# Rounded weight and remainder interleaved element by element in SBUF

## The chip, the core and the metric

The kernel runs on one core of a Trainium2 chip. The metric is device time in microseconds of one execution; lower is better. A core has five engines with queues of their own: TensorE (PE) multiplies matrices, and loads its weights by separate instructions, which the profile lists as PEld; VectorE (DVE), ScalarE (ACT) and GpSimd (POOL) work element by element on 128 partitions; SyncE (SP) here only issues DMA transfers. SBUF is the on-chip memory that all of them read, PSUM takes the results of TensorE.

## What is computed

One layer of a decoder for 256 prompt tokens and 8 single decode tokens, together 264 columns, with a model width of 2048 and a feed-forward width of 5632. Everything is fp32.

```python
x = x + concat(RGLRU_group(xn), mLSTM_group(xn)) @ w_out      # xn = rmsnorm(x); inputs from xn @ w_in
xq = rmsnorm(x, g_xa) @ w_xa_q                                # cross attention, 4 heads, 256 memory tokens
s  = einsum('blhd,bmhd->bhlm', xq, mk) * 512 ** -0.5          # prompt: mk = mn @ w_k, mv = mn @ w_v
x  = x + (softmax(s) @ mv) @ w_xa_o                           # decode: mk, mv from caches
xf = rmsnorm(x, g_ffn)
x  = x + (silu(xf @ w_ffn_gate) * (xf @ w_ffn_up)) @ w_ffn_down
y  = rmsnorm(x, g_final)
```

The states of the two groups and the memory's keys and values are outputs too. Most of the arithmetic is in the projections, the products with w_in, w_out, w_xa_q, w_k, w_v, w_xa_o, gate, up and down.

## The kernel before

Activations lie with the features on the partitions: a chunk is 128 features by 264 tokens. The weight is the stationary operand of a projection, a block of 128 by 128 numbers, and the activations stream past it. TensorE multiplies fp32 in one pass only in a rounded format (fp32r), so each operand is split in two: a rounded part (h) and a remainder (l). `mm3` (line 179) then makes three matmuls for each chunk, weight h by activation h, weight h by activation l, weight l by activation h, and each of them loads its weights anew.

The program is a list `steps`. One step is usually one output block of 128 features: 2048 weights on each partition (16 blocks of 128), one DMA of 1 MB into `raw` (three buffers, issued by SP three steps ahead), a split, 48 matmuls into one PSUM bank. `split_half` (line 150) splits 1024 columns of the next step: ScalarE copies them to `wh`, which rounds, and VectorE subtracts `wh` from `raw` into `wl`. `wh` and `wl` are separate tiles with four buffers each, so the halves of two steps are in SBUF. `W` (line 169) hands `mm3` the 128 columns of a block from both tiles, contiguous in each. The very first step is split in parts of 256 and 512 columns. In the last part of the down projection a step has 1536 columns, and its second half 512.

Two kinds of step differ. `split_gates` and `pe_if` (lines 506 and 517) take only 64 columns of each block, put rounded part and remainder side by side in one block, and use each block for two matmuls. `pe_v` (line 1034) computes the memory's values with tokens on the partitions: there activations are the weights of the array and w_v, in pieces of 512 columns, is the moving operand; it has 16 steps.

Beside the projections runs side work, written as generators (`rg_gen`, `ml_gates`, `ml_heads`, `dec_k`, `dec_v`, `attend` and others), which `pump` advances between steps by estimated engine clocks. A scheduler then sets the order on PE, VectorE, ScalarE and POOL; the splits have high priority. SP's order is as written. POOL issues the DMAs of the caches (`kcT`, `vcT`, lines 966 and 970) and of outputs, and makes one subtraction (line 977) for each decode token and head.

The stages follow in this order: w_in (41 steps, gates among them), w_out (16), w_q (16), for each of four heads w_k (4) and w_v (4), w_o (16), gate and up (88), down (48, in three parts between them). Nearly all instructions are recorded under line 60, a helper's, so they are told apart by tiles: `mm<-B,wh` is a matmul with a rounded weight into a bank named mm. The small operations that the prediction uses are `evac_rgx` (line 407, eight numbers written with a step of four elements), `evac_q` (line 946, eight adjacent ones into `qsm`), and the two writers of `den` (lines 697 and 732, two adjacent numbers, and four with a step of three).

Of the kernel before, what the change touches and what calls it, by code (L numbers as in the profile page):

```python
# [10 lines left out]
F32 = mybir.dt.float32  # L11
F32R = mybir.dt.float32r
I32 = mybir.dt.int32
AF = mybir.ActivationFunctionType
# [3 lines left out]
P = 128  # L18
# [62 lines left out]
def layer_kernel(ctx: ExitStack, tc, xT, memT, vec, wrg, w_in, w_out, w_q, w_k, w_v, w_o,  # L81
# [3 lines left out]
    act, dve, pe = Engine(nc.scalar, price_act), Engine(nc.vector, price_dve), Engine(nc.tensor, price_pe)  # L85
# [3 lines left out]
    sb = ctx.enter_context(tc.tile_pool(name="sb", bufs=1))  # L89
# [6 lines left out]
    def nm(s):  # L96
        uid[0] += 1
        return f"{s}_{uid[0]}"

    def B(shape, dt=F32):  # L100
        return sb.tile(shape, dt, tag="B", bufs=NB, name=nm("B"))
# [35 lines left out]
    steps = []  # L137
    LD, LS = 3, 1

    raws, splits = {}, {}  # L140

    def load_piece(i):
        if i >= len(steps) or i in raws:
# [6 lines left out]
    def split_half(i, h, parts=1):  # L150
        if i >= len(steps):
            return
        if steps[i][2] is pe_if:
            if h == 0:
                split_gates(i)
            return
        cols = steps[i][1]
        lo, hi = h * 1024, min(cols, (h + 1) * 1024)
        wh = sb.tile([P, 1024], F32R, tag="wh", bufs=4, name=nm("wh"))
        wl = sb.tile([P, 1024], F32R, tag="wl", bufs=4, name=nm("wl"))  # L160
        r = raws[i]
        n = (hi - lo) // parts
        with tc.high_priority():
            for o in range(0, hi - lo, n):
                st["split"] = act.activation(wh[:, o: o + n], r[:, lo + o: lo + o + n], AF.Copy)
                dve.tensor_sub(wl[:, o: o + n], r[:, lo + o: lo + o + n], wh[:, o: o + n])
        splits[i, h] = (wh, wl)

    class W:
        def __init__(self, i):  # L170
# [15 lines left out]
    st = {}  # L186
# [48 lines left out]
    def bank(tag="mm"):  # L235
        return psm.tile([P, 512], F32, tag=tag, bufs=4, name=nm(tag))
# [269 lines left out]
    def split_gates(i):  # L506

        r = raws[i]
        for h in range(2):
            w = sb.tile([P, 8, P], F32R, tag="wh", bufs=4, name=nm("wh"))  # L510
            x = r[:, h * 1024: h * 1024 + 1024].rearrange("p (c m) -> p c m", m=P)
            with tc.high_priority():
                act.activation(w[:, :, 0:64], x[:, :, 0:64], AF.Copy)
                dve.tensor_sub(w[:, :, 64:128], x[:, :, 0:64], w[:, :, 0:64].bitcast(F32))
            splits[i, h] = w
# [303 lines left out]
    def proj(src, rhs, evac, cols=2048, n=N, need=()):  # L819

        def f(i):
            ps = bank()
            w = W(i)
            nch = cols // P
            for c in range(nch):
                mm3(ps[:, :n], w(c), rhs(c), c == 0, c == nch - 1)
            return ps
        steps.append((src, cols, f, evac, need))
# [191 lines left out]
    def evac_k(h, j):  # L1020
        def f(ps):
            if j == 0:
                kv["k", h] = HL(4, T)
            t = tmp(T)
            act.activation(t, ps[:, :T], AF.Copy)
            pool_e.dma_start(o_k[:, 4 * h + j, :], t)
            kh, kl = kv["k", h](j)
            act.activation(kh, ps[:, :T], AF.Copy)
            dve.tensor_sub(kl, ps[:, :T], kh.bitcast(F32))
            if j == 3:  # L1030
                st["att", h] = side(attend(h), 1)
        return f

    def pe_v(h, k4):
        def f(i):
            if k4 == 0:
                kv["vps"] = [bank(), bank()]
            w = W(i)
            for c in range(4):
                kc = k4 * 4 + c  # L1040
                mh, ml_ = rm(kc)
                wh, wl = w(c, 512)
                for tb in range(2):
                    ps = kv["vps"][tb]
                    s = slice(tb * P, tb * P + P)
                    pe.matmul(ps, mh[:, s], wh, start=(kc == 0), stop=False)
                    pe.matmul(ps, mh[:, s], wl, start=False, stop=False)
                    pe.matmul(ps, ml_[:, s], wh, start=False, stop=(kc == KC - 1))
            return kv["vps"]
        return f  # L1050

    def evac_vm(h):
        def f(vps):
            vv = B([P, 2, 512], F32R), B([P, 2, 512], F32R)
            kv["v", h] = vv
            vf = B([P, 2, 512])
            for tb in range(2):
                vh = vv[0][:, tb, :]
                act.activation(vh, vps[tb], AF.Copy)
                dve.tensor_sub(vv[1][:, tb, :], vps[tb], vh.bitcast(F32))  # L1060
                act.activation(vf[:, tb, :], vps[tb], AF.Copy)
                pool_e.dma_start(o_v[tb * P: tb * P + P, h * 512: h * 512 + 512], vf[:, tb, :])
            kv["vn"] = h + 1
        return f
# [57 lines left out]
    for h in range(H):  # L1122
        for j in range(4):
            proj(w_k[4 * h + j], rm, evac_k(h, j), n=T, need=("memg",))
        for k4 in range(4):
            steps.append((w_v[h, k4], 2048, pe_v(h, k4), evac_vm(h) if k4 == 3 else None, ()))

    def ro(c):
        return st["o"](c)
# [84 lines left out]
    r = sb.tile([P, 2048], F32, tag="raw", bufs=3, name=nm("raw"))  # L1214
# [10 lines left out]
    with tc.high_priority():  # L1225
        for c in range(KC):
            split(*xn(c), xres[:, c, :], V("g_mix", c))
            if c == 1:
                split_half(0, 0, 4)
            elif c == 3:  # L1230
                split_half(0, 1, 2)

    pend = []
    for i, (src, cols, pef, evf, need) in enumerate(steps):
# [12 lines left out]
        now = pe.clock  # L1247
        dve.clock, act.clock = max(dve.clock, now), max(act.clock, now)
        split_half(i + LS, 0)
        if i + LS < len(steps) and steps[i + LS][1] > 1024:  # L1250
            split_half(i + LS, 1)
# [17 lines left out]
    for lo, hi in ((0, 1), (1, 2), (2, 4), (4, 6), (6, 8), (8, 10), (10, 12), (12, 14), (14, 16)):  # L1269
        for c in range(lo, hi):  # L1270
            e, r = (pool_e, rstd) if c in POOLC else (dve, fin["ps"][:, :N])
# [108 lines left out]
```

## Time and profile before

| | |
|---|---|
| median of 2 runs | 1575.51 us (1574.54 and 1576.49) |
| the profiled execution's own time | 1576.51 us |
| its span, first to last instruction | 1574.8 us |
| mean granted TensorE clock | 0.991 |
| PE, PEld busy | 1556.5 us, 1532.6 us |
| VectorE, ScalarE busy | 1051.4 us, 789.7 us |
| rounding of weights on ScalarE, 1024 columns | 494 times, 1060 ns |
| remainder on VectorE, 1024 columns | 494 times, 1226 ns |

A group's row reads: line, engine, operation, output and inputs by name, shapes, count; then busy time in us and the mean of one in ns; then the engine's idle time before them and who ended it. Matmuls are pipelined: the record of one is longer than the distance to the next, so the pace is read from counts in a stretch, and records are only compared with each other. A row of a stretch gives its length, then for PE, PEld, VectorE, ScalarE and POOL the busy time with the number of instructions, then the granted clock, the DMA engines' share, and GB/s.

### The profile page before, as it was taken

The page shows a single profiled execution, that of the slowest core. Times are in us where ns is not written, and L with a number is a line of the kernel's source. Part 1 is how long each engine was busy: PE and PEld are TensorE (multiplying, and loading weights), DVE is VectorE, ACT ScalarE, POOL GpSimd, SP SyncE. Part 2 cuts the span into 40 slices and gives each one's busy share as a digit, 9 for nine tenths or more (in the row PEclk, how much of TensorE's full clock was granted, in tenths as well). Part 3 has the DMA queues.
Part 4 walks back from the last instruction along what each step waited for, and adds up shares of the span by engine and source line. Part 5 has one row for each costly group of instructions (what it writes and reads, how often), then busy time and mean ns, then how long its engine had stood idle before and what let it go on. Part 6 is the DMA issues. An engine that isn't in the chain of part 4 may idle for free.

```text
span 1574.8 us, 29829 instructions
## 1 busy us (share of the span) xinstructions
PE 1556.5 (99%) x12340; PEld 1532.6 (97%) x12340; DVE 1051.4 (67%) x2021; ACT 789.7 (50%) x1252; POOL 109.6 (7%) x174
## 2 busy tenths in 40 slices
PE   9999999999999999999999999999999999999997
PEld 8999999999999889999999999999999999999997
DVE  7876877787699899956655555455555554555554
ACT  7465675565455656645444444333444433344463
POOL 0001210000124333200000000000000000000000
PEclk9999999999999999999999999999999999999998
DMA  8455875546689788745545555555455554555452
GB/s 304 161 174 172 294 269 205 178 145 245 248 321 346 302 305 319 251 161 178 187 164 185 188 180 175 181 188 186 174 179 186 187 181 172 184 188 184 156 179 99
DMA packets 55303, 325.97 MB, mean 207 GB/s; under 512 B 6688, under 2 KB 7120, under 8 KB 24448
## 3 DMA queue, kind: packets, MB, share of 16 engines
q1 hardware_dynamic: 39744, 270.68, 48.4%
q0 software_dynamic: 15136, 53.16, 9.4%
q8 instruction: 96, 1.57, 0.4%
q14 instruction: 39, 0.32, 0.1%
q10 hardware_dynamic: 288, 0.23, 0.1%
HBM read 312.78 MB, written 11.28 MB: 206 GB/s over the span
## 4 chain that ended last, share of the span: by engine, by line
PE 94%; DMA 2%; DVE 2%; ACT 1%; issue 1%; DVEq 0%; POOL 0%; SPq 0%; ACTq 0%
PE mm L60 89%; PE ax L60 4%; DVE B L60 1%; DMA o_sc<-B 1%; ACT B L60 1%; DMA raw<-w_in 1%; ACT wh L60 0%; DMA B<-scr 0%; DVE wl L60 0%; ACT L60 0%; DMA vecs<-vec 0%; DMA scr<-lt 0%; DVE t L60 0%; DVE dw L60 0%; ACT t L60 0%
## 5 line engine op out<-in xcount | busy, mean ns | idle before, releaser
L60 PE MATMUL mm<-B,wh 128*128 128x264 f32 (+1 forms) x7520 | 1379.0, 285 | 4.8 <-DVE B L60 3.0
L60 PEld LDWEIGHTS mm<-B,wh 128*128 128x128 f32 x7520 | 1168.4, 189 | 6.4 <-ACT cso L60 3.1
L60 PE MATMUL mm<-B,wl 128*128 128x264 f32 (+1 forms) x3744 | 1062.8, 284 | 0.6 <-DVE wl L60 0.6
L60 ACT ACTIVATE wh<-raw 128x1024 fp32r<-128x1024 f32 (+2 forms) x518 | 536.9, 1038 | 692.0 <-PE mm L60 574.6
L60 DVE TENSOR_TENSOR wl<-raw,wh 128x1024 fp32r<-128x1024 f32 (+2 forms) x516 | 619.0, 1201 | 356.7 <-ACT wh L60 350.0
L60 PEld LDWEIGHTS mm<-B,wl 128*128 128x128 f32 x3744 | 706.7, 189 | 1.1 <-DVE wl L60 1.0
L60 DVE TENSOR_TENSOR t<-mm,rstd 128x264 f32<-128x264 f32 x104 | 44.9, 432 | 60.2 <-PE mm L60 60.2
L60 PE MATMUL mm<-wh,B 128*128 128x512 f32 x256 | 82.3, 395 | 0.0
L60 DVE TENSOR_TENSOR xres<-xres,mm 128x264 f32<-128x264 f32 x80 | 34.2, 428 | 47.1 <-PE mm L60 47.1
L1272 POOL TENSOR_TENSOR B<-B,rstd 128x264 f32<-128x264 f32 x4 | 2.8, 743 | 864.9 <-ACT rstd L60 864.9
L60 PEld LDWEIGHTS mm<-wh,B 128*128 128x128 f32 x256 | 47.8, 189 | 9.8
L60 DVE SCALAR_TENSOR_TENSOR B<-B,dw 128x256 f32<-128x256 f32 x128 | 52.6, 465 | 2.3 <-ACT dw L60 2.3
L60 PE MATMUL mm<-wl,B 128*128 128x512 f32 x128 | 50.6, 395 | 0.0
L60 DVE SCALAR_TENSOR_TENSOR dw<-B,qsm,dw 128x256 f32<-128x256 f32 x96 | 47.9, 500 | 1.4 <-ACT dw L60 0.7
L60 PE MATMUL ax<-B,B 128*128 128x256 f32 (+3 forms) x288 | 48.2, 308 | 0.3 <-DVE B L60 0.3
L60 PEld LDWEIGHTS ax<-B,B 128*128 128x128 f32 x288 | 40.8, 189 | 4.0 <-issue 1.2
L977 POOL TENSOR_TENSOR ds<-dw,ds 128x256 fp32r<-128x256 f32 x32 | 35.4, 1107 | 115.3 <-ACT ds L60 115.2
L60 ACT ACTIVATE B<-xres,vecs 128x264 fp32r<-128x264 f32 (+1 forms) x64 | 31.1, 503 | 2.5 <-DMA xres<-xT 1.4
L60 ACT ACTIVATE t<-xres 128x264 f32<-128x264 f32 x60 | 23.9, 413 | 15.4 <-DVE xres L60 15.4
L60 PEld LDWEIGHTS mm<-wl,B 128*128 128x128 f32 x128 | 24.1, 188 | 5.0
L966 POOL DMA_DIRECT2D B<-kcT x32 | 17.5, 546 | 147.4 <-DVE B L60 127.0
L60 DVE TENSOR_TENSOR acc_x<-acc_x,t 128x264 f32<-128x264 f32 x59 | 25.2, 428 | 0.9 <-ACT t L60 0.5
(157 smaller groups left out, 740.0 us busy)
## 6 DMA issues: line engine op xcount, KB each, us to landing
raw<-w_gu SPq DMA_DIRECT2D x88, 1024.0 KB, 4.8
raw<-w_in SPq DMA_DIRECT2D x40, 1024.0 KB, 4.9
raw<-w_d SPq DMA_DIRECT2D x32, 1024.0 KB, 4.8
raw<-w_out SPq DMA_DIRECT2D x16, 1024.0 KB, 4.8
B<-kcT POOLq DMA_DIRECT2D x32, 512.0 KB, 6.1
raw<-w_q SPq DMA_DIRECT2D x16, 1024.0 KB, 5.0
B<-vcT POOLq DMA_DIRECT2D x32, 512.0 KB, 7.2
raw<-w_k SPq DMA_DIRECT2D x16, 1024.0 KB, 6.4
```

Of the source, the lines that this page charges most:

```text
L60: return f(*a, **k)
L966: pool_e.dma_start(kc, kcT[h, b])
L977: pool_e.tensor_sub(ws[:, 1], acc, ws[:, 0].bitcast(F32))
L1272: e.tensor_mul(st["y"](c), st["y"](c), r)
```

## The change

`wh` and `wl` become one tile `w` of 2048 columns with four buffers, in which rounded part and remainder alternate: element 2k is the rounded part of weight k, element 2k + 1 its remainder. ScalarE writes every second element, VectorE reads the rounded part at a step of two elements and writes its result at a step of two, and each weight load for `mm3` takes 128 elements out of 256, a step of 8 bytes. The steps of w_v are marked `wide` and keep two contiguous parts in the tile. The gates keep their contiguous blocks, in the first half of a tile. The space is the same: four buffers of 8 KB a partition in place of four and four of 4 KB.

```diff
-    raws, splits = {}, {}
+    raws, splits, wide = {}, {}, set()
...
-        wh = sb.tile([P, 1024], F32R, tag="wh", bufs=4, name=nm("wh"))
-        wl = sb.tile([P, 1024], F32R, tag="wl", bufs=4, name=nm("wl"))
+        wt = wtile()
         r = raws[i]
+        if i in wide:
+            splits[i, h] = wt[:, 0:1024], wt[:, 1024:2048]
+            with tc.high_priority():
+                act.activation(wt[:, 0:1024], r[:, lo: hi], AF.Copy)
+                dve.tensor_sub(wt[:, 1024:2048], r[:, lo: hi], wt[:, 0:1024].bitcast(F32))
+            return
+
+        wt = wt.rearrange("p (k t) -> p k t", t=2)
+        wh, wl = wt[:, :, 0], wt[:, :, 1]
         n = (hi - lo) // parts
         with tc.high_priority():
             for o in range(0, hi - lo, n):
-                st["split"] = act.activation(wh[:, o: o + n], r[:, lo + o: lo + o + n], AF.Copy)
-                dve.tensor_sub(wl[:, o: o + n], r[:, lo + o: lo + o + n], wh[:, o: o + n])
+                xo = r[:, lo + o: lo + o + n]
+                st["split"] = act.activation(wh[:, o: o + n], xo, AF.Copy)
+                dve.tensor_sub(wl[:, o: o + n], xo, wh[:, o: o + n].bitcast(F32))
         splits[i, h] = (wh, wl)
+
+    def wtile():
+        return sb.tile([P, 2048], F32R, tag="w", bufs=4, name=nm("w"))
...
-            w = sb.tile([P, 8, P], F32R, tag="wh", bufs=4, name=nm("wh"))
+            w = wtile()[:, 0:1024].rearrange("p (c m) -> p c m", m=P)
...
         for k4 in range(4):
             steps.append((w_v[h, k4], 2048, pe_v(h, k4), evac_vm(h) if k4 == 3 else None, ()))
+            wide.add(len(steps) - 1)
```

The number of instructions on each engine stays the same, 12195 on PE among them, and SP's order too. The scheduler moves a few rows on the other engines. On PE, the first place is the transposes of the gates' columns (`ax<-ident`), which stand between the matmuls of two steps of w_in. Before:

```order
L60 MATMUL ax_1661<-B_884,ident 128x16 x3
L60 MATMUL ax_1661<-ident,B_966 128x4 x2
L60 MATMUL mm_1600<-B_126,wh_1520 128x264
L60 MATMUL mm_1600<-B_127,wh_1520 128x264
L60 MATMUL ax_1661<-ident,B_966 128x4 x3
L60 MATMUL ax_1749<-ident,B_1284 128x128 x4
L60 MATMUL mm_1528<-B_162,wl_1443 128x264
```

And now:

```order
L60 MATMUL ax_1623<-B_866,ident 128x16 x3
L60 MATMUL ax_1623<-ident,B_946 128x4 x3
L60 MATMUL mm_1562<-B_126,w_1486 128x264
L60 MATMUL mm_1562<-B_127,w_1486 128x264
L60 MATMUL ax_1623<-ident,B_946 128x4 x2
L60 MATMUL ax_1709<-ident,B_1256 128x128 x4
L60 MATMUL mm_1492<-B_160,w_1409 128x264 x2
```

One transpose of the five has moved ahead of the two matmuls of the next step.

On POOL, the place is the stage of w_k and w_v, where the caches of the decode tokens are loaded (`kcT`, `vcT`) and the decode queries' products are split (`ds`). Before:

```order
L966 DMA B_5847<-kcT 128x1024
L977 TENSOR_TENSOR ds_5601<-dw_5600,ds_5601 128x256
L970 DMA B_5851<-vcT 128x1024
L977 TENSOR_TENSOR ds_5684<-dw_5683,ds_5684 128x256
L966 DMA B_5936<-kcT 128x1024
L970 DMA B_5940<-vcT 128x1024
L966 DMA B_6019<-kcT 128x1024
L977 TENSOR_TENSOR ds_5767<-dw_5766,ds_5767 128x256
```

And now:

```order
L978 DMA B_5707<-kcT 128x1024
L989 TENSOR_TENSOR ds_5467<-dw_5466,ds_5467 128x256
L982 DMA B_5711<-vcT 128x1024
L989 TENSOR_TENSOR ds_5548<-dw_5547,ds_5548 128x256
L989 TENSOR_TENSOR ds_5629<-dw_5628,ds_5629 128x256
L978 DMA B_5794<-kcT 128x1024
L982 DMA B_5798<-vcT 128x1024
L978 DMA B_5875<-kcT 128x1024
```

One subtraction has moved ahead of the loads of the next pair. What follows from such pairs on VectorE stands up to two steps earlier or later from there on, and at the same step as before again towards the end of the stage.

## The prediction

> **What bounds the kernel now.** I read the page's engine table and its chain first, then the groups of instructions with their shapes kept apart, then a table by stretch of the span, and last the timeline of a microsecond where weight loads can be seen without long matmuls beside them. The page:
>
> ```profile
> span 1574.8 us, 29829 instructions
> PE 1556.5 (99%) x12340; PEld 1532.6 (97%) x12340; DVE 1051.4 (67%) x2021; ACT 789.7 (50%) x1252; POOL 109.6 (7%) x174
> PE 94%; DMA 2%; DVE 2%; ACT 1%; issue 1%; DVEq 0%; POOL 0%; SPq 0%; ACTq 0%
> ```
>
> TensorE is the bound: matmuls are under way in 99% of the span, and 94% of the chain that ended last lies on PE. But PEld, the weight loads, is at 97% too, so the page does not yet say whether a matmul's stream or the load in front of it sets the pace. The reader should see in the next rows what one of each takes.
>
> ```profile
> L60 PE MATMUL mm<-B,wh 128*128 128x264 f32 x7008 | 1286.0, 285 | 4.1 <-DVE B L60 3.0 <-ACT wh L60 1.1
> L60 PE MATMUL mm<-B,wh 128*128 128x256 f32 x512 | 93.1, 281 | 0.6 <-ACT B L60 0.5
> L60 PE MATMUL mm<-wh,B 128*128 128x512 f32 x256 | 82.3, 395 | 0.0
> ...
> L60 PEld LDWEIGHTS mm<-B,wh 128*128 128x128 f32 x7520 | 1168.4, 189 | 6.4 <-ACT cso L60 3.1 <-ACT wh L60 1.4 <-ACT B L60 1.1
> L60 PEld LDWEIGHTS mm<-B,wl 128*128 128x128 f32 x3744 | 706.7, 189 | 1.1 <-DVE wl L60 1.0
> ...
> L60 PEld LDWEIGHTS ax<-B,wh 128*128 128x128 f32 x64 | 10.8, 208 | 2.5 <-ACT wh L60 2.0 <-DVE B L60 0.2
> L60 PEld LDWEIGHTS ax<-B,wl 128*128 128x128 f32 x32 | 6.3, 203 | 0.0
> ```
>
> ```profile
> 760.00:1550.00 790.00, 790.00 (x6527) 790.00 (x6526) 435.43 (x543) 336.47 (x408) 0.00 (x0) 1.00 0.51 179
> ```
>
> That stretch (in order: us, PE, PEld, DVE, ACT and POOL busy, each with its instructions, clock, DMA share) holds W_o and the feed-forward part. 790 us over 6527 matmuls is one every 121.0 ns. From 256 to 512 columns a matmul grows from 281 to 395 ns, 0.445 ns a column; 264 columns stream for 117 ns. So the stream explains 117 of the 121 ns. What the load needs shows where the matmuls between loads are one column long:
>
> ```profile
> 37.55 0.76 PEld L60 LDWEIGHTS ax<-ones,acc_x 128*128 128x128 f32 x6
> 37.67 0.72 PE L60 MATMUL ax<-ones,acc_x 128*128 128x1 f32 x6
> ```
>
> Six loads run in 0.76 us, and one record is 0.19 us long, so they start (0.76 - 0.19) / 5 = 0.114 us apart with nothing to stream. A weight load of 128 contiguous fp32 columns therefore takes up to 114 ns, and it lies under a stream of 117 ns in a slot of 121. Both are nearly equal; the load has about 7 ns to spare. That is the point on which this change turns.
>
> **The change, part by part.** It adds and removes no instruction. It alters the address pattern of three kinds.
>
> First, the weight loads. Strided are all loads of projections: the four rows above give 7520 + 3744 + 64 + 32 = 11360, less 32 of the gates' step (16 chunks, two matmuls each), whose weights stay contiguous: 11328. The 384 matmuls that take W_v as the moving operand read contiguous halves as before. Each load now steps 2 elements, 8 bytes. No load in the trace has such a step, so I bound it. From below: nothing, for it is hidden unless it grows by over 7 ns, and a gain is limited to what the stream does not explain, 121 - 117 = 4 ns, 45 us over all loads. From above, the nearest rows are small VectorE operations that differ in the step of the result alone: the same product of PSUM and rstd, written to adjacent places (qsm), and to every fourth element (the history rows of line 407, "B").
>
> ```profile
> L60 DVE TENSOR_TENSOR qsm<-mm,rstd 128x8 f32<-128x8 f32 x16 | 2.5, 154 | 0.0
> L60 DVE TENSOR_TENSOR B<-mm,rstd 128x8 f32<-128x8 f32 x6 | 1.0, 160 | 0.0
> ```
>
> 6 ns over 8 elements is 0.75 ns an element with a step of 16 bytes. On 128 weights that is 96 ns, so the load would need 210 and each slot would grow by 210 - 121 = 89 ns: 11328 x 0.089 = 1008 us. Against it stands a ScalarE pair, two adjacent elements and four with a step of 12 bytes:
>
> ```profile
> L60 ACT ACTIVATE den<-ax 128x2 f32<-128x2 f32 x4 | 0.6, 160 | 0.3 <-PE ax L60 0.3
> L60 ACT ACTIVATE den<-ax 128x4 f32<-128x4 f32 x1 | 0.2, 156 | 0.0
> ```
>
> There the step costs nothing that can be seen. A step of 8 bytes is nearer to 12 than to 16, and a load takes one element in 114 / 128 = 0.89 ns, against 0.445 ns an element on the moving operand: the load asks for half the bytes a nanosecond that TensorE is seen to read, so skipping every second element brings its address span only to what the stream already does. I take 0 for the load, and keep both ends.
>
> [...]
>
> Second, ScalarE's rounding writes every second element, and third, VectorE's remainder reads its second input and writes its result so.
>
> ```profile
> L60 ACT ACTIVATE wh<-raw 128x1024 fp32r<-128x1024 f32 x494 | 523.0, 1060 | 674.8 <-PE mm L60 562.8 <-issue 94.4 <-ACT B L60 12.4
> L60 DVE TENSOR_TENSOR wl<-raw,wh 128x1024 fp32r<-128x1024 f32 x494 | 605.2, 1226 | 355.8 <-ACT wh L60 349.0
> ```
>
> 462 of the 494 of each become strided (32 are halves of W_v). Bounds again 0 and 0.75 ns an element: 0 or 0.77 us an operation. ScalarE waits 675 us in front of these operations, mostly for a buffer that TensorE gives back, 1.4 us ahead of each: 0.77 us fits in that wait. On VectorE the cover differs by stretch:
>
> ```profile
> 40.00:250.00 210.00, 205.09 (x1546) 199.78 (x1545) 164.80 (x441) 128.93 (x266) 23.23 (x43) 0.95 0.64 218
> 250.00:400.00 150.00, 150.00 (x1242) 150.00 (x1241) 116.84 (x220) 86.94 (x142) 2.11 (x4) 1.00 0.53 190
> 400.00:480.00 80.00, 80.00 (x664) 80.00 (x663) 64.96 (x163) 40.68 (x61) 18.91 (x27) 1.00 0.76 284
> 480.00:560.00 80.00, 79.87 (x582) 75.52 (x581) 71.75 (x185) 47.71 (x89) 26.44 (x38) 1.00 0.87 328
> 560.00:640.00 80.00, 79.48 (x493) 71.14 (x492) 76.46 (x207) 50.92 (x106) 27.50 (x40) 1.00 0.84 311
> ...
> 40.00:250.00 210.00, 126.55 (x434) 84.50 (x433) 66.74 (x55) 0.95 0.64 218
> 250.00:400.00 150.00, 112.92 (x399) 74.91 (x400) 61.03 (x50) 1.00 0.53 190
> 400.00:480.00 80.00, 60.34 (x214) 40.06 (x214) 31.89 (x27) 1.00 0.76 284
> 480.00:560.00 80.00, 53.93 (x180) 33.72 (x179) 32.97 (x27) 1.00 0.87 328
> 560.00:640.00 80.00, 43.65 (x131) 24.47 (x130) 29.40 (x25) 1.00 0.84 311
> ```
>
> The second block is the same stretches for instructions on wl alone; its third pair is VectorE's remainders. At the upper bound VectorE would need 165 + 55 x 0.77 = 207 of 210 us, 155 of 150, 86 of 80, 93 of 80 and 96 of 80: 5 + 6 + 13 + 16 = 40 us too much. In the feed-forward stretch 435 of 790 us leave room for all of its remainders. At half the bound only the last two stretches overflow, by 2 and 6 us. By the nearer row I take 0.
>
> The rest: wh and wl share a buffer, so ScalarE's next half waits for the last reader of either, which is one matmul (0.12 us) later than before; the 1.4 us of waiting hide it. VectorE no longer waits for TensorE itself, since ScalarE has done so for the same buffer. The scheduler moves a few rows: in the gates' transposes one 4-column transpose goes ahead of two matmuls, at a place where PE waits for VectorE's remainder as it is; in the K and V projections the caches' loads on POOL's queue and what follows from them move by a step or two, and SP's order is the same. The wait at the transposes is this row's:
>
> ```profile
> 128.88 0.59 PE L60 MATMUL mm<-B,wl 128*128 128x264 f32 x1 [0.64 <-DVE wl L60]
> ```
>
> A step is 48 x 0.121 = 5.8 us, but nothing at the end of the stage moves, so I cost these at 0. Their cover is the PE work of that stretch (79.5 of 80 us busy); without it a cache load that comes late would show as PE idle.
>
> The sum is 0 + 0 + 0 against the profiled execution, 1576.5 us with a span of 1574.8 and 1.7 us around it; it stands 1 us over the median of 1575.5. I say 1578, with a microsecond or two for reshuffled rows.
>
> **Rivals.** (1) The strided load is slower and becomes the bound, on the other side of my forecast. Its place is every projection matmul, its price 11.3 us for each nanosecond beyond the 7 to spare: 2% (32 us) are reached 2.8 ns further, at a load of 124 ns. At the upper bound the time is 1577 + 1008 = 2585 us, at half of it 11328 x (114 + 48 - 121) ns = 464, so 2041. For it: the load has so little to spare, and the 160 against 154 ns. Against it: 12-byte steps that cost nothing, and the moving operand's rate. [...] The rows here show its cost at 16 bytes and no run shows it at 8. I give it 16%.
>
> (2) The load stays hidden, and VectorE or ScalarE write slower. Then VectorE overflows where it is over 80% busy, with 8 us at half the bound and 40 at the whole: 1585 to 1616 us. For it: 96% busy in 560 to 640 us. Against: den. 12%.
>
> (3) A gain: if the 4 ns between stream and slot come from loads that disturb streams, and the new pattern does not, up to 45 us: 1532. Nothing in the rows points to the pattern as their cause. 4%.
>
> (4) That nothing really becomes strided, so that the change does not do what it says, gives my own time; the program's tiles are interleaved, so I fold it into the forecast.
>
> **How the numbers follow.** No change in what is hidden: 68%, at 1578. With rival 2, 80%: the range is 1560 to 1620, from a gain of 1% (a third of the gain that rival 3 allows) to the upper end of rival 2. It leaves out rival 1 and most of rival 3. Over 2% (32 us, about what a measurement of this kernel tells from no change) slower: rival 1 and, of rival 2, the part over 1607 us with cases between the two, 26% together. Faster by over 2%: 4%. Within: 70%.
>
> **What would show it.** Right: the 264-column matmul still at 285 ns, a matmul every 121 ns in the stretch of the feed-forward part, remainder and rounding at 1226 and 1060 ns. The load's record need not stay at 189 ns for the time to stay. Wrong by rival 1: the matmul's record grows with the slot (about 210 ns from start to start), with VectorE and ScalarE idle behind it. Wrong by rival 2: remainders over 1.6 us, PE waiting for VectorE in 480 to 640 us. [...]

## The result and the profile after

The changed kernel takes 1596.68 us (median of 2 runs, 1596.17 and 1597.18) against 1575.51: a ratio of 1.013, with a 95% interval of 1.009 to 1.018. That is 21 us more. It lies inside the range and within 2%, but the interval leaves out 1, so the kernel became slower, while the forecast's sum had no term that grew. The profiled execution is the one of 1597.18 us.

The page of the changed kernel, its span, its engines and its chain by engine:

```profile
span 1595.4 us, 29784 instructions
...
PE 1576.3 (99%) x12340; PEld 1553.1 (97%) x12340; DVE 1052.2 (66%) x2021; ACT 827.7 (52%) x1252; POOL 109.7 (7%) x174
...
PE 97%; ACT 1%; DVE 1%; DMA 0%; issue 0%; SPq 0%; DVEq 0%; ACTq 0%
```

The span grew by 20.6 us and PE's busy time by 19.8, at the same 12340 matmuls. So PE does not wait more; its work became longer. VectorE's busy time moved by 0.8 us, ScalarE's grew by 38.

The groups with shapes kept apart (mean ns of one after the comma). All 11328 strided matmuls and their loads now carry the name `w` (with the 32 of the gates), and `w,B` are the W_v matmuls, whose operands stayed contiguous:

```profile
L60 PEld LDWEIGHTS mm<-B,w 128*128 128x128 f32 x11264 | 1396.8, 197 | 7.4 <-ACT cso L60 3.3 <-DVE w L60 1.7 <-ACT w L60 1.3
L60 PE MATMUL mm<-B,w 128*128 128x264 f32 x10496 | 1311.2, 287 | 5.9 <-DVE B L60 3.2 <-DVE w L60 1.5 <-ACT w L60 1.2
L60 DVE TENSOR_TENSOR w<-raw,w 128x1024 fp32r<-128x1024 f32 x494 | 605.1, 1226 | 404.5 <-ACT w L60 403.2
L60 ACT ACTIVATE w<-raw 128x1024 fp32r<-128x1024 f32 x494 | 565.3, 1146 | 666.2 <-PE mm L60 489.4 <-issue 156.8 <-ACT B L60 11.7
L60 PE MATMUL mm<-w,B 128*128 128x512 f32 x384 | 92.7, 395 | 0.0
L60 PEld LDWEIGHTS mm<-w,B 128*128 128x128 f32 x384 | 70.7, 189 | 14.9
```

The strided load's record went from 189 to 197 ns, the 264-column matmul's from 285 to 287; the W_v matmuls kept 395 and 189 ns. VectorE's remainder is unchanged at 1226 ns, ScalarE's rounding is 86 ns longer. ScalarE still waits 666 us in front of its roundings, so these 86 ns are paid in its own idle time.

The feed-forward stretch, where PE is never idle (us, then PE, PEld, DVE, ACT and POOL busy with their instructions):

```profile
760.00:1550.00 790.00, 790.00 (x6426) 790.00 (x6426) 428.28 (x529) 349.00 (x396) 0.00 (x0) 1.00 0.51 177
```

The same 790 us hold 6426 matmuls in place of 6527: one in 122.9 ns in place of 121.0. Over 11328 strided matmuls 1.9 ns are 21.5 us, the whole difference. What had to be found is which part of the change makes the slot longer, and how, since the prediction took a load that fits under the slot to cost nothing.

### The profile page after: what moved, and what is told of

Read it like the earlier page. It is cut to its first block, busy times and chain, and to the rows that moved or that the text cites. A ratio compares the mean times of both kernels' runs of the same rounds, so it can differ in the third digit from the quotient of the medians.

```text
span 1595.4 us, 29784 instructions
## 1 busy us (share of the span) xinstructions
PE 1576.3 (99%) x12340; PEld 1553.1 (97%) x12340; DVE 1052.2 (66%) x2021; ACT 827.7 (52%) x1252; POOL 109.7 (7%) x174
## 4 chain that ended last, share of the span: by engine, by line
PE 97%; ACT 1%; DVE 1%; DMA 0%; issue 0%; SPq 0%; DVEq 0%; ACTq 0%
PE mm L60 92%; PE ax L60 5%; DVE B L60 1%; ACT B L60 1%; DMA xres<-xT 0%; ACT L60 0%; ACT w L60 0%; DVE w L60 0%; DVE c L60 0%; DVEq L1370 0%; DVE xres L60 0%; ACT t L60 0%; SPq L1232 0%; ACT rstd L60 0%; SPq L1225 0%
## 5 line engine op out<-in xcount | busy, mean ns | idle before, releaser
L60 PE MATMUL mm<-B,w 128*128 128x264 f32 (+1 forms) x11264 | 1407.3, 287 | 6.0 <-DVE B L60 3.2
L60 PEld LDWEIGHTS mm<-B,w 128*128 128x128 f32 x11264 | 1396.8, 197 | 7.4 <-ACT cso L60 3.3
L60 ACT ACTIVATE w<-raw 128x1024 fp32r<-128x1024 f32 (+2 forms) x518 | 580.2, 1122 | 681.2 <-PE mm L60 499.9
L60 DVE TENSOR_TENSOR w<-raw,w 128x1024 fp32r<-128x1024 f32 (+2 forms) x518 | 620.4, 1199 | 405.5 <-ACT w L60 404.2
L60 PE MATMUL mm<-w,B 128*128 128x512 f32 x384 | 92.7, 395 | 0.0
L60 PEld LDWEIGHTS mm<-w,B 128*128 128x128 f32 x384 | 70.7, 189 | 14.9
L60 DVE SCALAR_TENSOR_TENSOR B<-xres,vecs,B 128x264 fp32r<-128x264 f32 x48 | 22.7, 490 | 5.5 <-ACT B L60 5.5
L60 ACT ACTIVATE t<-t 128x264 f32<-128x264 f32 (+1 forms) x61 | 24.9, 408 | 0.1
L60 ACT ACTIVATE dw<-B,qsm 128x256 f32<-128x256 f32 x32 | 16.2, 508 | 15.2 <-DVE B L60 9.0
L60 ACT ACTIVATE t<-B,B 128x128 f32<-128x128 f32 x64 | 21.5, 392 | 0.6 <-DMA B<-scr 0.6
```

Source lines behind the costliest of these rows:

```text
L60: return f(*a, **k)
```

## The experiments

Three explanations were open at the start: the stepping weight loads make each slot longer; ScalarE's and VectorE's strided accesses disturb TensorE's reads; the common tile and the rows that moved with it cost the time.

### Only the loads stepped

The kernel before, its two tiles and its writes stay as they are. The weights are laid out in HBM so that the blocks of two neighbouring chunks alternate element by element; `W` then picks every second of 256 elements.

```diff
             wh, wl = splits[self.i, c // per]
+            if w == P:
+                q, j = divmod(c % per, 2)
+                o = q * 2 * P
+                return tuple(x[:, o: o + 2 * P].rearrange("p (k t) -> p k t", t=2)[:, :, j] for x in (wh, wl))
...
-        "w_out": _blocks(f("w_out")[0]),
+        "w_out": _mix(_blocks(f("w_out")[0])),
```

> The kernel before, with the blocks of two neighbouring chunks interleaved by the layout of the weights in HBM, so that rounded part and remainder are written contiguously to two separate tiles as before, and only the weight loads step two elements. If the strided load lengthens every slot (my theory, 1.9 ns on 11328 matmuls): 1597 us, a load's record of 197 ns, a 264-column matmul every 123 ns, the rounding at 1060 ns. If the strided writes of ScalarE or the moved rows cost the 21 us: 1576 us and 121 ns.

It took 1595.61 us against 1575.26, ratio 1.013 [1.011, 1.015]. The groups of its loads and roundings, and its feed-forward stretch:

```profile
L60 PEld LDWEIGHTS mm<-B,wh 128*128 128x128 f32 x7520 | 1200.5, 196 | 5.8 <-ACT cso L60 3.1 <-ACT B L60 1.0 <-ACT wh L60 0.9
L60 ACT ACTIVATE wh<-raw 128x1024 fp32r<-128x1024 f32 x494 | 523.1, 1060 | 696.1 <-PE mm L60 580.3 <-issue 96.4 <-ACT B L60 13.2
```

```profile
760.00:1550.00 790.00, 790.00 (x6428) 790.00 (x6428) 427.76 (x531) 329.33 (x397) 0.00 (x0) 1.00 0.50 177
```

The load pattern alone gives the whole difference: the load's record is at 196 ns, the rounding at its old 1060, and the stretch holds 6428 matmuls, two from the changed kernel's 6426.

### Only the writes stepped

The changed kernel, with `W` handing out contiguous halves of the tile.

```diff
-        splits[i, h] = (wh, wl)
+        splits[i, h] = (ws[:, 0: hi - lo], ws[:, hi - lo: 2 * (hi - lo)])
```

> The changed kernel with its strided writes and reads on ScalarE and VectorE, but each weight load takes 128 adjacent elements of the interleaved tile, so the projections multiply by a mixture of rounded parts and remainders and their values are not the layer's. If the load is the cause: 1576 us, a load's record of 189 ns, 121 ns a matmul, the rounding still at 1146 ns. If the writes are the cause: 1597 us with a load's record of 189 ns. If both have a share, something between.

1576.21 us, ratio 1.0006 [0.9997, 1.0016]. Its loads and roundings, and the stretch:

```profile
L60 PEld LDWEIGHTS mm<-B,w 128*128 128x128 f32 x11264 | 1375.5, 189 | 6.7 <-issue 2.9 <-DVE w L60 2.6 <-ACT B L60 0.3
...
L60 ACT ACTIVATE w<-raw 128x1024 fp32r<-128x1024 f32 x494 | 562.0, 1139 | 640.4 <-PE mm L60 466.2 <-issue 155.0 <-ACT B L60 12.3
```

```profile
760.00:1550.00 790.00, 790.00 (x6518) 790.00 (x6518) 435.20 (x541) 354.50 (x408) 0.00 (x0) 1.00 0.51 179
```

The rounding is about as long as in the changed kernel (1139 ns against 1146), and the slot is back at 121.2 ns. Each load takes 128 adjacent elements of the interleaved tile, so the products are not the layer's, with the same number and shapes of instructions. The strided writes cost TensorE nothing that can be measured.

### One tile, blocks of 128

The common tile, the four buffers and the moved rows of the change, but rounded part and remainder alternate in blocks of 128 and every access is contiguous.

```diff
-        wt = wt.rearrange("p (k t) -> p k t", t=2)
-        wh, wl = wt[:, :, 0], wt[:, :, 1]
+        wt = wt.rearrange("p (c t m) -> p c t m", t=2, m=P)
+        wh, wl = wt[:, :, 0, :], wt[:, :, 1, :]
```

> The changed kernel with one tile for both parts, but interleaved in blocks of 128 columns, so that every load is contiguous and ScalarE and VectorE write runs of 128. It keeps the common buffer and the scheduler's order of the change. If the access patterns are the cause: 1576 us and the rounding at 1060 ns. If the common buffer or the moved rows cost it: 1597 us.

1575.0 us, ratio 0.9999 [0.9989, 1.001]. The tile and the moved rows cost nothing. With the two runs before it this leaves the loads alone.

### The load by itself

Behind the end of the kernel before stand rows of 24 matmuls with the same weights each, at a step of 1, 2, 3, 4 and 8 elements (`sa` to `se`), with 8 columns to stream and then with 264. This part comes on top of the kernel's time, so only its rows are read.

```diff
+    for k, s in enumerate((1, 2, 3, 4, 8)):
+        x = sb.tile([P, P * s], F32R, tag="B", bufs=NB, name=f"s{'abcde'[k]}")
+        act.activation(x, y3[:, 0: P * s], AF.Copy)
+        sx.append(x if s == 1 else x.rearrange("p (k t) -> p k t", t=s)[:, :, 0])
...
+    for n in (8, 264, 8, 264):
+        for x in sx:
+            for _ in range(24):
+                pe.matmul(ps[:, :n], x, warmer[:, :n], start=True, stop=True)
```

> The kernel before with loads measured by themselves behind its end, when no other engine works: 24 matmuls each with weights at a step of 1, 2, 3, 4 and 8 elements (tiles sa to se), first with 8 columns moving, so that the loads set the pace, then with 264, all of it twice. If a strided load takes longer: with 8 columns 112 ns at a step of 1 and some 120 at 2 (the record grew by 8 ns), more at 3, and at 4 and 8, one element in 16 bytes or fewer, up to the 210 ns of the prediction's upper bound; with 264 columns 121 ns at a step of 1, 123 at 2. If the load itself is not longer and the stream beside it is disturbed by other engines' traffic: 112 ns at 1 and 2 alike, and no difference with 264 columns either, since nothing else runs.

The stretches of this part first (the granted clock is the third number from the end), then the loads in order of time (start, length, count). The granted clock is 1.00 up to 1585 us and 0.50 from 1586 us on, some 4 us after the 8-column matmuls begin at 1581.8 us, and 1.00 again from 1610 us, so the lengths at full clock are read from before 1585 us and from 1610 to 1630 us. The rows shown from before 1600 us stream 8 columns, those from 1610 to 1628 us 264, and the last one 8 again.

```profile
1575.00:1585.00 10.00, 10.00 (x88) 10.00 (x87) 0.00 (x0) 0.00 (x0) 0.00 (x0) 1.00 0.00 0
1586.00:1609.00 23.00, 23.00 (x103) 23.00 (x104) 0.00 (x0) 0.00 (x0) 0.00 (x0) 0.50 0.00 1
1610.00:1630.00 20.00, 20.00 (x113) 20.00 (x111) 0.00 (x0) 0.00 (x0) 0.00 (x0) 1.00 0.00 1
```

```profile
1581.82 2.77 PEld L60 LDWEIGHTS mm<-warmer,sa 128*128 128x128 f32 x24
1584.50 4.32 PEld L60 LDWEIGHTS mm<-warmer,sb 128*128 128x128 f32 x24
...
1593.83 5.70 PEld L60 LDWEIGHTS mm<-warmer,sd 128*128 128x128 f32 x24
1599.43 5.80 PEld L60 LDWEIGHTS mm<-warmer,se 128*128 128x128 f32 x24
...
1610.01 2.95 PEld L60 LDWEIGHTS mm<-warmer,sb 128*128 128x128 f32 x24
1612.89 4.24 PEld L60 LDWEIGHTS mm<-warmer,sc 128*128 128x128 f32 x24
1617.04 5.69 PEld L60 LDWEIGHTS mm<-warmer,sd 128*128 128x128 f32 x24
1622.64 5.90 PEld L60 LDWEIGHTS mm<-warmer,se 128*128 128x128 f32 x24
1628.44 3.87 PEld L60 LDWEIGHTS mm<-warmer,sa 128*128 128x128 f32 x24
```

From one group's start to the next, over 24, a load takes 112 ns at step 1 (2.68 us), 120 in a slot at step 2 (2.88), 173 at step 3, 233 at step 4 and 242 at step 8. The number of elements is always 128, so they are not what the growth is paid for: from step 2 to step 4 it goes with the span that is read, and then hardly any further. Steps 3 and 4 take 58 ns for each element of the step (173 / 3 and 233 / 4). By the author's estimate from these two a load at step 2 needs 116 ns, and 120 were measured; at step 1 it gives 58 ns, so the span is not the limit of the 112 ns there. So at step 2 the load has, by this estimate, just become bound by its span, at about the length of the slot. At half the granted clock (0.50) the load at step 4 takes the same 233 ns (5.60 us from 1593.83 on), so its pace at this step does not follow TensorE's clock.

### Step 4 in the whole kernel

The same kernel as the first experiment, with four neighbouring chunks alternating.

```diff
-                q, j = divmod(c % per, 2)
-                o = q * 2 * P
+                q, j = divmod(c % per, 4)
+                o = q * 4 * P
```

> [...] If a load's cost depended on the elements alone, 1597 us as at a step of 2.

2845.78 us in a single run. The matmuls with rounded weights in this kernel:

```profile
L60 PE MATMUL mm<-B,wh 128*128 128x264 f32 x7008 | 2212.9, 398 | 2.9 <-DVE B L60 2.9
```

1271 us over the kernel before, or 112 ns for each of 11328 matmuls, as much as lies between the slot of 121 ns and the 233 ns of the load measured alone: the load sets the slot, as it did alone. The matmul's record grows from 285 to 398 ns with it, though its stream did not change.

### The slot against the columns

Rows of 24 matmuls behind the end again, with 128 to 320 columns, weights contiguous (`wa`) and at step 2 (`wb`), and longer streams between them so that the clock stays whole.

```diff
+        for n in (128, 224, 248, 256, 264, 280, 320):
+            go(wa, one, n)
+            go(wb, two, n)
+            rest()
```

> The kernel before with matmuls measured behind its end, alone on the chip: weights contiguous (wa) and at a step of two elements (wb), with 128, 224, 248, 256, 264, 280 and 320 columns moving, then triples as the projections make them from contiguous tiles (wha, wla) and interleaved ones (whb, wlb); all three times. If a slot is the longer of load and stream: up to about 250 columns a flat 112 ns contiguous and 118 strided, from 264 on no difference, and the triples alike at 121. If the strided load also disturbs the stream that it lies under: a difference of some 2 ns at 264, 280 and 320 columns too, and 123 against 121 in the triples, with no other engine at work. If it takes the other engines' traffic: triples alike here, and only the kernel shows the 2 ns.

The timeline of the matmuls (start, length, count):

```profile
1655.80 2.79 PE L60 MATMUL mm<-mh,wa 128*128 128x128 f32 x24
1658.42 3.04 PE L60 MATMUL mm<-mh,wb 128*128 128x128 f32 x24
1661.30 3.12 PE L60 MATMUL mm<-warmer 128*128 128x264 f32 x24
...
1681.26 3.01 PE L60 MATMUL mm<-mh,wa 128*128 128x256 f32 x24
1684.11 3.07 PE L60 MATMUL mm<-mh,wb 128*128 128x256 f32 x24
1687.02 3.05 PE L60 MATMUL mm<-warmer 128*128 128x264 f32 x24
1689.91 3.13 PE L60 MATMUL mm<-mh,wa 128*128 128x264 f32 x24
1692.87 3.10 PE L60 MATMUL mm<-mh,wb 128*128 128x264 f32 x24
1695.81 3.05 PE L60 MATMUL mm<-warmer 128*128 128x264 f32 x24
...
1707.79 3.68 PE L60 MATMUL mm<-mh,wa 128*128 128x320 f32 x24
1711.31 3.71 PE L60 MATMUL mm<-mh,wb 128*128 128x320 f32 x24
1714.86 3.04 PE L60 MATMUL mm<-warmer 128*128 128x264 f32 x24
```

Start to start, over 24: at 128 columns 109 ns contiguous (112 between the single matmuls inside the row) and 120 at step 2; at 256 columns 119 and 121; at 264 columns 123 and 122; at 320 columns 147 and 148. The strided load puts a floor of 120 ns under the slot. But with 264 columns, at these addresses, the contiguous slot is already 123 ns, above that floor, and the strided load makes it 1 ns shorter; with 320 columns, 27 ns above the floor, it makes it 1 ns longer. Triples as the projections make them, in the same run, took 121.7 ns contiguous and 122.3 at step 2.

A floor under each single slot does not make 121 into 123 either. In the kernel before, the starts of its 264-column matmuls from 800 to 1540 us lie 117 to 125 ns apart in nine of ten cases, and 24% of these slots are shorter than 120 ns. Lifting every one of them to 120 would bring 0.5 of the 1.9 ns. So the two reads must act on each other, or addresses matter.

### One kind of load stepped

First only the remainders' loads, one of the three in each triple (the layout in HBM is undone by ScalarE's read, and VectorE reads the rounded part with a step of 128 elements), then only those of the rounded parts, two of three (undone by VectorE).

```diff
+                return wh[:, k: k + P], wl[:, o: o + 2 * P].rearrange("p (k t) -> p k t", t=2)[:, :, j]
```

> As load_step2, but only the remainders' loads step two elements: ScalarE reads the interleaved weights at a step of two and writes the rounded parts in order, so the rounded parts' loads are contiguous. A third of the 11328 loads is strided. If the price is one of each strided load by itself (1.9 ns): 1575 + 7 = 1582 us, and of the three slots of a triple only the one under which a strided load lies is longer. If the stretched slots come from a common rhythm of all loads: either no change (1575 us) or over 1585.

1588.65 us, ratio 1.0084 [1.0065, 1.0103]. The feed-forward stretch of this kernel:

```profile
760.00:1550.00 790.00, 790.00 (x6462) 790.00 (x6461) 442.56 (x535) 350.44 (x399) 0.00 (x0) 1.00 0.51 178
```

A third of the loads bring 13.8 us, two thirds of the whole; a price per strided load would have brought a third of it. The mean slot is 122.25 ns. From 800 to 1540 us all three slots of a triple are longer than in the kernel before, by 0.9, 1.2 and 1.6 ns.

The second of the two, with the roles of `wh` and `wl` exchanged in `W`:

```diff
+                v = lambda y: y.rearrange("p (q k t) -> p q k t", t=2, k=P)
+                dve.tensor_sub(wl[:, o: o + n].rearrange("p (q t k) -> p q t k", t=2, k=P), v(x),
+                               v(wh[:, o: o + n]))
...
+                return wh[:, o: o + 2 * P].rearrange("p (k t) -> p k t", t=2)[:, :, j], wl[:, k: k + P]
```

> The counterpart of wl_step2 (1588.7 us): the rounded parts' loads, two thirds of all, step two elements, the remainders' loads are contiguous, and VectorE writes the remainders back in order; ScalarE writes as before. If each strided load costs the same, 1575 + 14 = 1589 us, and wl_step2 was too dear by its strided reads on ScalarE. If a strided load shifts the rhythm of its neighbours too, as the three slots of wl_step2 show (0.9 to 1.6 ns each), the price saturates: 1590 to 1596 us, near that of all loads (1595.6).

1629.72 us, ratio 1.0348 [1.033, 1.0365], far over what was expected. The edit brought a cost of its own, since VectorE now writes its remainder with a step of 128 elements; the group of the remainders, and a table by stretch:

```profile
L60 DVE TENSOR_TENSOR wl<-raw,wh 128x1024 fp32r<-128x1024 f32 x494 | 993.1, 2013 | 186.2 <-ACT wh L60 179.8
```

```profile
480.00:560.00 80.00, 73.56 (x536) 69.37 (x535) 78.32 (x170) 40.41 (x71) 24.59 (x34) 1.00 0.85 315
560.00:640.00 80.00, 76.46 (x498) 69.92 (x497) 76.63 (x176) 42.64 (x86) 25.91 (x34) 0.98 0.73 266
760.00:1550.00 790.00, 790.00 (x6463) 790.00 (x6462) 636.81 (x535) 326.93 (x388) 0.00 (x0) 1.00 0.50 179
```

The remainder takes 2013 ns in place of 1226, 0.77 ns an element. VectorE is at 98% from 480 to 560 us, and PE, which was busy for 79.87 of these 80 us before, falls to 73.56. So the total says nothing on the loads. The feed-forward stretch does, for there VectorE has room: 6463 matmuls, the same as with a third of the loads strided. One third and two thirds each give 1.2 of the 1.9 ns, and the effect does not add up load by load. The write with a step of 128 elements may have had a part in that; this was not separated.

### Triples without the kernel around them

Four steps' worth of real triples behind the end, contiguous and at step 2 in turn; then the same with the moving operand broadcast from a single column, which leaves the loads and the number of columns, but has the stream read one place of SBUF.

```diff
+            if not wide:
+                bh, bl = (x[:, 0:1].to_broadcast([P, N]) for x in (bh, bl))
```

> The kernel before with whole steps repeated behind its end, alone on the chip: weights in four pairs of halves in the buffers of wh and wl, activations in tiles of four chunks, 48 matmuls a step, contiguous and at a step of two elements in turn, four times each; then the same with the moving operand broadcast from one column, so that the stream reads one place of SBUF. If the 2 ns come from load and stream inside TensorE and its reads of SBUF: 121 against 123 ns a slot, as in the kernel, with no other engine at work. If it takes the other engines' or the DMA's traffic: 121 against 121. With the broadcast: if stream and load collide in SBUF, contiguous and strided both fall to their own pace, 117 or less against 118 to 120; if the collision is not in SBUF, no change from the first part.

Three matmuls of `ones` part the steps of 48 (plain fp32, each in two records, so x6, where an fp32r matmul has one), so the distances between these rows of the timeline are one step each:

```profile
1626.64 0.83 PE L60 MATMUL mm<-ones 128*128 128x128 f32 x6
1633.15 0.83 PE L60 MATMUL mm<-ones 128*128 128x128 f32 x6
1639.69 0.83 PE L60 MATMUL mm<-ones 128*128 128x128 f32 x6
1645.76 0.83 PE L60 MATMUL mm<-ones 128*128 128x128 f32 x6
1652.09 0.83 PE L60 MATMUL mm<-ones 128*128 128x128 f32 x6
```

With real columns a step takes 6.51 us contiguous and 6.54 strided: 0.6 ns a slot. With one broadcast column it takes 6.07 and 6.33: 5.4 ns a slot. With the broadcast the contiguous step is 0.44 us shorter, 9 ns a slot, though it has the same loads and as many columns. Inside the steps the starts of the matmuls then lie 112 to 113 ns apart contiguous and 117 to 119 at step 2, nearly without spread: that is about what the loads take by themselves (112 and 120). With real columns they lie 116 to 127 ns apart. So reading 264 different columns has a price beside the loads, and the slot of 121 ns is not the load's length.

### The kernel's own last steps, repeated

The weights and activations of the down projection's last two steps are still in SBUF when the kernel ends. Their 72 matmuls are repeated six times at the same addresses, in the kernel before and in the one with only the loads stepped.

```diff
+    for _ in range(6):
+        for i in (len(steps) - 2, len(steps) - 1):
+            w = W(i)
+            for c in range(12):
+                mm3(ps[:, :N], w(c), st["a", 2](c), c == 0, c == 11)
+        for _k in range(2):
+            pe.matmul(ps[:, :P], st["y"](15)[:, 0:P], ones, start=True, stop=True)
```

> The kernel before with the matmuls of its last two steps repeated six times behind its end, from the same buffers at the same addresses, with no DMA and no other engine at work. Alone in triples_alone a contiguous slot took 121.7 ns and a strided one 122.4, a third of the kernel's difference, but at other addresses. If addresses set the rest: 121.0 ns a slot here, as in the kernel, and 123.0 in repeat_step2. If the traffic of other engines and of the DMA sets it: a difference of some 0.6 ns between the two.

> load_step2 with the same repetition. If addresses set the slot: 123.0 ns, as in the kernel at work. If traffic does: near the slot of repeat_contiguous, 0.6 ns above it.

The stretch of the repetitions and the matmuls that part them, contiguous:

```profile
1570.00:1634.00 64.00, 62.80 (x523) 62.61 (x521) 0.00 (x0) 0.00 (x0) 0.00 (x0) 1.00 0.00 1
```

```profile
1586.30 0.61 PE L60 MATMUL mm<-ones,B 128*128 128x128 f32 x4
1595.48 0.61 PE L60 MATMUL mm<-ones,B 128*128 128x128 f32 x4
1604.66 0.61 PE L60 MATMUL mm<-ones,B 128*128 128x128 f32 x4
```

And strided:

```profile
1595.00:1657.00 62.00, 61.83 (x511) 61.64 (x509) 0.00 (x0) 0.00 (x0) 0.00 (x0) 1.00 0.00 1
```

```profile
1609.73 0.60 PE L60 MATMUL mm<-ones,B 128*128 128x128 f32 x4
1619.03 0.60 PE L60 MATMUL mm<-ones,B 128*128 128x128 f32 x4
1628.33 0.60 PE L60 MATMUL mm<-ones,B 128*128 128x128 f32 x4
```

A repetition takes 9.18 us contiguous and 9.30 strided, every time. The 0.12 us over 72 matmuls are 1.7 ns each, while VectorE, ScalarE, POOL and the DMA engines do nothing. So nearly all of the 1.9 ns needs no other engine and no transfer: it arises in TensorE's own work. That it lies between its two reads, of weights and of columns, is argued from the broadcast column and not shown by this run.

### Another distance between activations

If the two reads act on each other through addresses, a contiguous kernel should feel them too. The kernel before, with 268 in place of 264 elements from one activation chunk to the next:

```diff
+                w = 268 if self.w == N else self.w
+                self.t[q] = B([P, min(4, self.nb), w], self.dt)[:, :, 0: self.w]
```

> [...] No instruction changes. In the repetitions alone the slot at each position of a step came out the same every time, so I take it that the addresses of load and stream set it. Then the 48 slots of a step get other lengths than the kernel's before (117 to 125 ns by position), and their mean moves by some tenths of a nanosecond to 2 ns either way: 1553 to 1597 us, with no sign foretold. If the slots are set by the instructions alone and not by addresses: the same 48 lengths and 1575 us.

1582.75 us, ratio 1.0043 [1.0026, 1.0059]. Its feed-forward stretch:

```profile
760.00:1550.00 790.00, 790.00 (x6492) 790.00 (x6491) 432.78 (x538) 333.27 (x403) 0.00 (x0) 1.00 0.50 179
```

No instruction and no step of a load differs from the kernel before, and yet the slot is 121.7 ns in place of 121.0: where the operands lie is worth 8 us by itself. None of the runs beats the kernel before.

## Why the prediction was right in its range and where it was off

**What bounds the kernel.** TensorE does, before and after: PE's busy time took 19.8 of the 20.6 us, and no wait grew enough to count. The load's pace of up to 114 ns from one-column matmuls stands at 112 in the separate measurement. The 117 ns for the stream are in doubt, and with them the 4 ns that were left over: with one broadcast column 264 columns and a load pass in 112.5 ns. What the stream takes with different columns and no load is not shown.

**The load, taken at 0 because it is hidden with 7 ns to spare.** This is the step that was off, in its size. The term is 11328 x 1.9 ns = 21.5 us. The load grew by some 8 ns (112 to 120). By the prediction's margin of 7 ns that is 1 ns a slot, about 11 us; set against the mean slot of 121 ns it is nothing. What the runs showed in place of that margin: load and stream are not independent. The slot of 123 ns is longer than the strided load's pace and longer than the contiguous slot. Rival 3 had a load disturb the stream beside it, but only as a gain, out of the 4 ns that were left over; the sum had no place for a load that fits under the stream and makes it slower. The bounds, 0 to 1008 us, held it near the lower end.

That 1596.7 us lies inside the range is luck, then: the upper end of 1620 was set for rival 2, which did not happen. Of the four signs of being right only the remainder's 1226 ns came; the matmul's record is 287 ns, the slot 122.9, the rounding 1146.

That a load which fits under the slot is free, as the term of 0 assumed, was the author's estimate; no row of before showed it. The repeated steps do not agree: 9.18 against 9.30 us with nothing but TensorE at work.

**Which row the price was taken from.** A step of 8 bytes was put nearer to the 12-byte step of `den`, which cost ScalarE nothing. For a load that neighbour misleads: step 3 costs it 61 ns (112 to 173). The argument from the moving operand's rate came nearer: 256 places at 0.445 ns are 114 ns, and 120 was measured. The far bound was nearer the truth in kind: 0.75 ns an element at 16 bytes gave a load of 210 ns, and 233 was measured.

**ScalarE and VectorE, taken at 0.** Right for the time. VectorE's remainder is at 1226 ns as before. ScalarE's rounding rose by 86 ns, 0.084 ns an element and a ninth of the upper bound; the wait in front of it hides that, and with strided writes alone the time was 1.0006 of before.

**The common buffer and the moved rows, taken at 0.** Right: 0.9999 with the tile and its order but contiguous accesses.

**The rivals.** The first, the load as the bound, did not happen at step 2 (a floor of 120 ns gives at most 0.5 of the 1.9 ns), but its mechanism and its signs are real: at step 4 the slot is the load's 233 ns, the matmul's record grows with it, and the time is 2846 us. It was set to begin at 7 ns of growth, and the measured growth stands right at that point. The second, VectorE overflowing in 480 to 640 us, did not happen either, but the run with writes 128 elements apart showed it at nearly the upper bound: 0.77 ns an element. Its 55 us, less the 13 to 14 us of slots that a run with the same mean slot paid, leave about 41 us; 40 was the figure. The match is in part chance: PE's idle time in that run grew by 27 us (from 18.3 to 45.4), and 8 of them lie from 40 to 250 us, where the prediction had still seen room. The third, a gain, found nothing for it: no pattern gave a shorter slot in the whole kernel.

**What stays open.** Why the strided load costs 1.7 to 1.9 ns at the kernel's addresses, 0.6 in the triples behind its end, and with one weight block used 24 times between 1 ns less (264 columns) and 1 ns more (320). The activation distance shows that addresses move the slot, but the rule by which they do was not tried. Nor is it shown whether the 9 ns that reading different columns costs come from the loads beside it or would be paid without loads, since each matmul here has a load.

## What to carry to other kernels

A weight load that is hidden under a stream of nearly its own length is not free to grow: ask how wide a span of SBUF it reads (alone it took 112, 120, 173 and 233 ns at steps of 1 to 4), and price a growth even where the load still fits: here it cost 1.9 ns a matmul in the kernel, times 11328, and 0.6 ns in the triples behind its end. At 4-byte elements a step of two cost 1.3% of this kernel and a step of four 81%, while the same step of two on VectorE cost nothing (1226 ns a remainder before and after); price each engine's access by a row of that engine. Where a stretch is bound by TensorE alone, compare the count of matmuls in equal windows: 6426 against 6527 showed in one row what the records of 285 and 287 ns hardly do.

## What the runs showed of the hardware that was not expected

- A load of 128 fp32 columns takes 112, 120, 173, 233 and 242 ns at steps of 1, 2, 3, 4 and 8 elements.
- With the moving operand broadcast from one column, a contiguous slot falls by 9 ns, to the 112.5 ns of the load; the step of 48 falls from 6.51 to 6.07 us.
- A load of step 4 takes 233 ns at the full granted clock (1.00) and at half of it (0.50).
- Four elements more between activation chunks make a kernel with contiguous loads 0.4% slower.
- VectorE's 1024-element remainder takes 1226 ns both contiguous and with result and one input at a step of two, and 2013 ns with its writes 128 elements apart; with one input read 128 elements apart and contiguous writes it takes 1267 ns.
- The clock granted to TensorE stood at 0.50 from 1586 to 1609 and from 1631 to 1657 us of the run with loads by themselves, after 8-column matmuls without a gap had begun at 1581.8 and at 1628.4 us, and at 1.00 again from 1610 and 1658 us, with 264 columns; PE is shown as busy throughout (23.00 of 23.00 and 26.00 of 26.00 us).
